# Decode and recurrence step of the sample rows moved beside gating branch and output projection, and a third projection bank in the recurrence

## Chip, cores and metric

One core of one Trainium2 chip runs the whole program. The metric is the device time of one execution in microseconds (us), lower is better. All data are float32; a large matmul is made of three passes over float32r halves ("hi" and "lo").

## What is computed

One hybrid layer is applied to a prompt of 1024 rows (1024 wide) and to 8 sample rows, each a one-token step with its own caches. After an RMS norm, `w_in` projects to three branches: A, dilated attention (12 heads of 64); B, spatial gating; C, a gated linear recurrence (6 heads, state 128 x 128 each). Their outputs, gated by silu, are joined and projected by `w_out`, and the input is added.

```python
aq, ak, av, az, bu, bv, bz, cq, cf, ci, cz = _project(xs, ...)      # the 8 sample rows
o_a = _dilated_step(aq, ak, av, cache_k[l], cache_v[l])             # 12 heads over 2048 cached rows
o_b, vn_s = _sgu(bu, bv, ...)
o_c, S_s = _hgrn2(cq, cf, ci, lb, norm_g, state_hgrn[l])            # S = f*S + k v ;  o = q S
xs = _merge(xs, o_a, az, o_b, bz, o_c, cz, w_out[l])
```

The prompt's rows go through the same functions with full attention over the dilated patterns and a recurrence over 1024 steps.

## The kernel before

The work is written in one order: `attention()` (six pairs of heads), `hgrn()` (branch C), `sgu()` (branch B), `out_proj(U)`. A scheduler moves instructions across these borders on each engine; each engine then runs its list strictly in order, and a DMA issue on SP that has to wait holds up all that stand behind it. Buffers come from tagged pools; two uses of one tag share its buffers in turn.

Weights come in blocks of 256 columns (`load_w`, L191 on): four raw tiles from SP, a high half by ACT (L205), a low half by POOL (L206). There are four buffers for high halves and four for low ones (one block), six for raw tiles. `proj_T` and `proj_nat` run 24 matmuls into a PSUM bank for one group of rows. Projections take turns on two banks (`p_proj`); the attention's transposes, the decode and the steps use the one bank of the tag "tr" (`p_tr`, `p_dk`).

`hgrn()` (L781) loops over three pairs of heads. For each it projects the values (pi, `c_proj_i`), query and forget gate (pc, `c_proj_qf`) and the output gate (pcz, `c_proj_z`). `gate` (L149) and `c_proj_qf` turn projections into gates on DVE and ACT (L152 reads a bank on DVE). `c_head` (L664) then runs the recurrence in eight blocks of 128 steps: decays (G, H), products per level (T, L648 to L656), small matmuls lv and ls, masked copies into cmat (L723 to L730), the output po, the next state S (L741), a norm pn.

After each head come the sample rows' parts. `c_step(h)` (L763) loads for all 8 rows the value row, broadcast to 128 partitions (vb), and the state (ss), forms f*S + k v on DVE (L772 to L774), writes the new state out, and multiplies by the queries (pd) on PE; `to_columns` (L754) turns the result. `decode(p)` (L924) handles two attention heads of the sample rows: for each half of the rows it loads three tiles of cached keys (dk) and the query (dqb), multiplies and sums on DVE (L950, L951), takes the softmax over partitions by small transposes (pmx, pmb) and a sum (pdn), then loads three tiles of cached values per half (dv) and multiplies (pda). Its tiles and the steps' have the tag "pq" (five buffers).

`sgu()` projects bv, then for each half of the columns bz and bu, and mixes (mx). `out_proj` (L982) takes four blocks of 256 output columns; each has eight row blocks of 48 matmuls (po). The halves yh and yl of the joined rows are made anew in each block on ACT, DVE and POOL (L1047, L1048). The first rows' tiles y0 to y7 come from DRAM by SP (L1010), the rest as yb (L1016). The sample rows' own product (pon, pos) is spread over blocks 0 to 2, with the raw weights of the block that follows.

Of the kernel before, what the change touches and what calls it, by code (L numbers as in the profile page):

```python
# [8 lines left out]
F32 = mybir.dt.float32  # L9
# [82 lines left out]
def hybrid_step(tc, ins, outs, parts=("A", "D", "B", "C", "O"), dbg=None):  # L92
    nc = tc.nc
    dbg = dbg or {}
# [4 lines left out]
    def mm(out, lhsT, rhs, start, stop):  # L99
        nc.tensor.matmul(out, lhsT=lhsT, rhs=rhs, start=start, stop=stop)  # L100

    with tc.tile_pool(name="const", bufs=1) as cp, tc.tile_pool(name="sb", bufs=1) as sb, \
# [478 lines left out]
        def c_proj_qf(h):  # L581
            blk = load_w([(OFF_CQ + h * P, P), (OFF_CF + h * P, P)], f"cqf{h}")
            f, q, kk = inp(f"f{h}"), inp(f"q{h}"), inp(f"k{h}")
            for j, dst in ((1, kk), (0, q)):
                for c in range(3):
                    ps = p_proj(f"pc{h}_{j}_{c}")
# [18 lines left out]
            qw = small(f"qs{h}", 5 * NS, tag="qs", bufs=2)  # L605
            nc.gpsimd.memset(qw[:, 3 * NS:], 0.0)
            qs = qw[:, 0:3 * NS].rearrange("p (a b) -> p a b", a=3)
            for i, x in enumerate((q, f, kk)):
                nc.scalar.copy(qs[:, i, :], x[:, S:L])
            return q, f, kk, qw  # L610

        def c_proj_i(hp):
            blk = load_w([(OFF_CI + hp * NW, NW)], f"ci{hp}")
            st = proj_nat_s(blk, f"ci{hp}")
            nc.sync.dma_start(qkv_d[3, :, hp * NW:(hp + 1) * NW], st)
            V = [inp(f"V{hp}_{j}", (P, NT, P)) for j in range(2)]
            for g in range(4):
                ps = p_proj(f"pi{hp}_{g}").rearrange("p (a b) -> p a b", a=2)
# [6 lines left out]
        def c_proj_z(hp):  # L625
            blk = load_w([(OFF_CZ + hp * NW, NW)], f"cz{hp}")
            Z = [inp(f"cz{hp}_{j}") for j in range(2)]
            for j in range(2):
                for c in range(3):
                    ps = p_proj(f"pcz{hp}_{j}_{c}")  # L630
# [33 lines left out]
        def c_head(h, q, f, kk, qw, V, z, At, lmask, dmask):  # L664
# [89 lines left out]
        def to_columns(rows, nm):  # L754

            sb_ = pq(f"{nm}s", (P, 2, P))
            nc.scalar.copy(sb_, rows[:, 0:256].rearrange("p (a b) -> p a b", a=2))
            pt = p_tr(nm)
            for i in range(2):
                nc.tensor.transpose(pt[:, i * P:(i + 1) * P], sb_[:, i, :], ident)  # L760
            return pt[:, 0:256].rearrange("p (b c) -> p b c", c=32)

        def c_step(h, q, f, kk, qw):  # L763

            qs = qw[:, 0:3 * NS].rearrange("p (a b) -> p a b", a=3)
            pd = p_tr(f"pd{h}")
            for b4 in range(2):
                bs = slice(4 * b4, 4 * b4 + 4)
                vb, ss = (pq(f"{n}{h}_{b4}", (P, 4, P)) for n in ("vb", "ss"))
                nc.sync.dma_start(vb, qkv_d[3, bs, h * P:(h + 1) * P].partition_broadcast(P))  # L770
                nc.sync.dma_start(ss, st_in[h][:, bs])
# [3 lines left out]
                nc.sync.dma_start(st_new[h][:, bs], ss)  # L775
                for b_ in range(4):
                    b = 4 * b4 + b_
                    mm(pd[32 * b_:32 * b_ + 32, b4 * P:(b4 + 1) * P], qw[:, b:b + 32], ss[:, b_, :], True, True)
            nc.scalar.copy(osT[:, h, :], to_columns(pd, f"pdt{h}s")[:, :, 0])

        def hgrn():  # L781
# [5 lines left out]
            At = [(cm[:, 256 * j:256 * j + 256], cm[:, 512 + 64 * j:576 + 64 * j]) for j in range(2)]  # L787
            for hp in range(3):
# [6 lines left out]
                a = c_proj_qf(2 * hp + 1)  # L795
                c_head(2 * hp + 1, *a, V[1], Z[1], At, lmask, dmask)
                c_step(2 * hp + 1, *a)
                decode(2 * hp + 1)

            n = HC * NS  # L800
            sq = pq("ssq", (P, n))
            nc.scalar.activation(sq, osT.rearrange("p h b -> p (h b)"), AF.Square)
            pn = p_tr("pns")
            mm(pn[:, :n], ones, sq, True, True)
            nc.scalar.activation(sq, pn[:, :n], AF.Ln, scale=1.0 / P, bias=eps)
            nc.scalar.activation(sq, sq, AF.Exp, scale=-0.5)
            nc.vector.tensor_tensor(osT, osT, sq.rearrange("p (h b) -> p h b", b=NS), ALU.mult)
            nc.vector.tensor_tensor(osT, osT, gn[:, :, None].to_broadcast([P, HC, NS]), ALU.mult)
            nc.vector.tensor_tensor(ysT[:, 10:16, :], osT, zsT, ALU.mult)


        def sgu():
            triu = small("triu", P, bufs=1, tag="kg")
# [3 lines left out]
            for j in range(2):  # L817
                ps = p_tr(f"wtp{j}").rearrange("p (a b) -> p a b", a=4)
# [12 lines left out]
            rs = p_tr("rs").rearrange("p (a b) -> p a b", a=4)  # L831
# [7 lines left out]
            st6 = small("st6", NT * 12, bufs=1, tag="dsc").rearrange("p (t a b) -> p t a b", t=NT, a=2)  # L839
            for j in range(2):  # L840
# [3 lines left out]
                for g in range(4):  # L844
# [5 lines left out]
                    for i in range(2):  # L850
                        nc.vector.bn_stats(st6[:, 2 * g + i, j, :], dst[:, i, :])

# [27 lines left out]
            pst = p_tr("pst").rearrange("p (a b) -> p a b", a=4)  # L880
# [218 lines left out]
```

## Time and profile before

| | |
|---|---|
| runs, us | 1285.92 median (1281.75, 1285.92, 1287.93) |
| the profiled execution, us | 1280.37, of which the span from first to last instruction is 1278.6 |
| busy in the span, us | PE 1203.0, DVE 918.0, ACT 669.1, POOL 290.5 |
| granted TensorE clock, mean | 0.98 |

The span is the time between the first and the last instruction of that one execution; the runs' times are those of separate executions. PE is TensorE's matmuls, DVE VectorE, ACT ScalarE, POOL GpSimd, SP the engine that issues most transfers. "Busy" counts time in which an instruction of that engine was under way; a busy PE is not PE at its peak. Stretches are named by microseconds from the span's start: attention's last pair ends near 545, the recurrence's small matmuls run from 569 to 992, the gating branch to 1079, the output projection to the end.

### The profile page before, as it was taken

The numbers are of one execution on the slowest core, as the hardware profiler recorded it, in microseconds if no ns is written. First come the engines' busy times: TensorE is split into PE (matmuls) and PEld (weight loads), VectorE is DVE, ScalarE is ACT, GpSimd is POOL, SyncE is SP. The second block draws the span as 40 slices with busy tenths as digits, with TensorE's granted clock in tenths as the row PEclk, the third lists the DMA queues.
The fourth block names the chain that finished last, engine by engine and source line by source line (L and its number), as shares of the span: only waits on it lengthen the run. The fifth ranks groups of instructions, "written<-read, shape, count | busy, mean of one in ns | idle before, by whom it ended". The sixth has DMA issues, their size and how long they took to land.

```text
span 1278.6 us, 27722 instructions
## 1 busy us (share of the span) xinstructions
PE 1203.0 (94%) x10610; PEld 1116.9 (87%) x10610; DVE 918.0 (72%) x2424; ACT 669.1 (52%) x1512; POOL 290.5 (23%) x272
## 2 busy tenths in 40 slices
PE   3899999999999998998999889998999999999998
PEld 2799888998899988987988878887989899899998
DVE  3945888668875886789897898989796534654643
ACT  4445555765548455575445554665433252454543
POOL 3531202312203121122012121111011254122221
PEclk9999999999899998998999989999999999999999
DMA  6151222312223141042253515424243224521110
GB/s 229 35 164 34 65 56 79 108 38 66 69 69 100 42 120 50 22 110 79 68 156 92 136 42 146 128 80 114 80 141 98 84 79 138 190 82 43 63 47 29
DMA packets 165044, 114.17 MB, mean 89 GB/s; under 512 B 13944, under 2 KB 158992, under 8 KB 164912
## 3 DMA queue, kind: packets, MB, share of 16 engines
q1 hardware_dynamic: 157520, 110.28, 29.4%
q10 hardware_dynamic: 6816, 1.54, 0.6%
q8 instruction: 83, 1.36, 0.4%
q0 software_dynamic: 576, 0.58, 0.3%
q14 instruction: 49, 0.40, 0.1%
HBM read 84.47 MB, written 22.09 MB: 83 GB/s over the span
## 4 chain that ended last, share of the span: by engine, by line
PE 71%; DVE 15%; issue 5%; DMA 5%; ACT 3%; SPq 1%; POOL 0%; ACTq 0%; DVEq 0%; POOLq 0%
PE po L100 15%; PE pqk L100 10%; PE pv L100 9%; PE paz L100 5%; PE pi L100 4%; PE pbu L100 4%; PE pbz L100 4%; PE pcz L100 3%; PE pbv L100 3%; PE st L100 3%; PE pc L100 3%; DMA dk<-in_cache_k_dram 3%; PE s L100 2%; DVE T L654 1%; DVE T L648 1%
## 5 line engine op out<-in xcount | busy, mean ns | idle before, releaser
L100 PE MATMUL pqk<-wh_qk,h 128*128 128x256 f32 x768 | 154.9, 292 | 5.0 <-DVE sd_qk L274 1.3
L100 PE MATMUL pc<-h,wh_cqf 128*128 128x344 f32 x576 | 144.6, 331 | 10.0 <-DVE cz L152 8.8
L100 PE MATMUL po<-woh,yh 128*128 128x256 f32 x512 | 144.3, 282 | 0.2 <-ACT yh L1047 0.2
L100 PE MATMUL po<-woh,yl 128*128 128x256 f32 x512 | 144.4, 282 | 0.0
L100 PE MATMUL po<-wol,yh 128*128 128x256 f32 x512 | 143.7, 281 | 0.0
L100 PEld LDWEIGHTS pqk<-wh_qk,h 128*128 128x128 f32 x768 | 126.0, 195 | 14.3 <-issue 3.2
L100 PEld LDWEIGHTS pc<-h,wh_cqf 128*128 128x128 f32 x576 | 102.0, 193 | 13.1 <-DVE cz L152 9.6
L100 PE MATMUL pqk<-wl_qk,h 128*128 128x256 f32 x384 | 111.3, 290 | 0.0
L100 PEld LDWEIGHTS po<-woh,yl 128*128 128x128 f32 x512 | 96.4, 188 | 3.0 <-issue 1.7
L100 PEld LDWEIGHTS po<-woh,yh 128*128 128x128 f32 x512 | 96.5, 188 | 2.0 <-ACT yh L1047 2.0
L100 PEld LDWEIGHTS po<-wol,yh 128*128 128x128 f32 x512 | 96.5, 188 | 0.0
L100 PE MATMUL pc<-h,wl_cqf 128*128 128x344 f32 x288 | 95.1, 332 | 0.0
L456 DVE CUSTOM_DVE_ANT_0 s<-s,masks 128x512 f32<-128x512 f32 (+2 forms) x144 | 77.6, 576 | 19.0 <-PE s L100 17.8
L100 PE MATMUL pi<-wh_ci,h 128*128 128x256 f32 x384 | 79.4, 301 | 12.3 <-DVE cmat L723 8.1
L100 PEld LDWEIGHTS pi<-wh_ci,h 128*128 128x128 f32 x384 | 65.1, 204 | 15.3 <-ACT dsc L963 5.4
L100 PEld LDWEIGHTS pqk<-wl_qk,h 128*128 128x128 f32 x384 | 74.9, 195 | 1.3 <-issue 0.2
L100 PE MATMUL pv<-wh_v,h 128*128 128x256 f32 x384 | 73.7, 284 | 0.0
L100 PE MATMUL pcz<-h,wh_cz 128*128 128x344 f32 x288 | 71.3, 326 | 0.2 <-DVE q L152 0.2
L100 PE MATMUL paz<-h,wh_az 128*128 128x344 f32 x288 | 69.2, 323 | 0.0
L1048 DVE TENSOR_TENSOR yl<-yb,yh 128x512 fp32r<-128x512 f32 x44 | 30.2, 690 | 53.0 <-ACT yh L1047 53.0
L100 PEld LDWEIGHTS pv<-wh_v,h 128*128 128x128 f32 x384 | 60.7, 189 | 1.8 <-issue 0.7
L1047 ACT CAST yh<-yb 128x512 fp32r<-128x512 f32 x64 | 39.5, 620 | 43.0 <-PE po L100 43.0
(388 smaller groups left out, 3586.2 us busy)
## 6 DMA issues: line engine op xcount, KB each, us to landing
wro<-in_w_out_dram SPq DMA_DIRECT2D x32, 256.0 KB
wr_qk<-in_w_in_dram SPq DMA_DIRECT2D x48, 128.0 KB
wr_cqf<-in_w_in_dram SPq DMA_DIRECT2D x48, 128.0 KB
dk<-in_cache_k_dram SPq DMA_DIRECT2D x24, 192.0 KB
dv<-in_cache_v_dram SPq DMA_DIRECT2D x24, 192.0 KB
xt<-in_x_prompt_dram SPq DMA_DIRECT2D x8, 512.0 KB
xr<-in_x_prompt_dram SPq DMA_DIRECT2D x32, 128.0 KB
out_o_yp_dram<-xr SPq DMA_DIRECT2D x32, 128.0 KB
```

Of the source, the lines that this page charges most:

```text
L100: nc.tensor.matmul(out, lhsT=lhsT, rhs=rhs, start=start, stop=stop)
L456: nc.vector.tensor_tensor_reduce(out=ps[:, :w], in0=ps[:, :w], in1=nmask[:, S - n + c:S - n + c + w], op0=ALU.add, op1=ALU.max, scale=1.0, ...
L648: nc.vector.tensor_tensor(K.rearrange("p (n w) -> p n w", w=w), g3[:, :, w - 1:w].to_broadcast([P, 4 * n, w]), h3, ALU.subtract)
L654: nc.vector.tensor_tensor(Q[:, 0:3], Q[:, 0:3], q4[:, 1:4], ALU.mult)
L1047: nc.scalar.copy(yh[:, sl, :], y)
L1048: (nc.gpsimd if piece == 0 else nc.vector).tensor_tensor(yl[:, sl, :], y, yh[:, sl, :].bitcast(F32), ALU.subtract)
```

## The change

- **Sample rows move.** `c_step` and `decode` become generators (`c_steps`, `decodes`) cut into stages by `yield`. `stages` makes a function `point()` that advances both by one stage; it is called after each group of bv (8 times), of bz and bu (24 times) and after each row block of the output projection (32 times). A decode has eight stages; a step starts every third point from the ninth on. Their PE instructions are pinned behind what was written before them on PE; what is written later may still be put ahead.
- **Buffers.** The steps' tiles take the tag "s2" (six buffers), `to_columns` the tag "e"; decodes within the output projection take "big". A step's product and state update are done by ACT (`activation` with Copy and a scale) and one DVE instruction for each row. The decode's memsets go from POOL to DVE. The queries' columns of all heads lie in the mask tile.
- **Three banks.** In `hgrn` each third projection group takes the bank "tr" (`p_turn`). The output gate pcz is projected before pc.
- **Output.** The sample rows' product is made in blocks 2 and 3 of the projection; for blocks 0 and 1 the raw weights are loaded again in block 3 (16 transfers of 256 KB), and block 3's own weights are loaded from the fourth row pair on.

The core of the diff:

```diff
+        def p_turn(nm):
+            turn[0] += 1
+            return p_tr(nm) if turn[0] % 3 == 0 else p_proj(nm)
...
-        def c_step(h, q, f, kk, qw):
-            pd = p_tr(f"pd{h}")
-            for b4 in range(2):
-                vb, ss = (pq(f"{n}{h}_{b4}", (P, 4, P)) for n in ("vb", "ss"))
...
-                nc.vector.tensor_tensor(vb, vb, qs[:, 2, bs, None].to_broadcast([P, 4, P]), ALU.mult)
-                nc.vector.tensor_tensor(ss, ss, qs[:, 1, bs, None].to_broadcast([P, 4, P]), ALU.mult)
-                nc.vector.tensor_tensor(ss, ss, vb, ALU.add)
...
+        def c_steps(qs):
+            for _ in range(8):
+                yield
+            for h in range(HC):
+                X = []
+                for b4 in range(2):
+                    vb, ss = (s2(f"{n}{h}_{b4}", shape=(P, 4, P)) for n in ("vb", "ss"))
+                    nc.sync.dma_start(vb, qkv_d[3, bs, h * P:(h + 1) * P].partition_broadcast(P))
+                    nc.sync.dma_start(ss, st_in[h][:, bs])
+                    for b_ in range(4):
+                        nc.scalar.activation(vb[:, b_, :], vb[:, b_, :], AF.Copy, scale=qs[:, 2, h, b:b + 1])
+                        nc.vector.scalar_tensor_tensor(ss[:, b_, :], ss[:, b_, :], qs[:, 1, h, b:b + 1], vb[:, b_, :],
+                                                       ALU.mult, ALU.add)
+                    nc.sync.dma_start(st_new[h][:, bs], ss)
+                yield
+                yield
+                pd = p_pv(f"pd{h}")
...
+                        pin(mm(pd[32 * b_:32 * b_ + 32, b4 * P:(b4 + 1) * P], qf[:, c:c + 32], X[b4][:, b_, :], True, True))
+                yield
+                nc.scalar.copy(osT[:, h, :], to_columns(pd, f"pdt{h}s", p_pv)[:, :, 0])
...
             for hp in range(3):
                 V = c_proj_i(hp)
-                a = c_proj_qf(2 * hp)
                 Z = c_proj_z(hp)
-                c_head(2 * hp, *a, V[0], Z[0], At, lmask, dmask)
-                c_step(2 * hp, *a)
-                decode(2 * hp)
...
+                for j in range(2):
+                    h = 2 * hp + j
+                    a = c_proj_qf(h, qs)
+                    c_head(h, *a, V[j], Z[j], At, lmask, dmask)
...
         def decode(p):
-            nc.gpsimd.memset(sc, NEG)
+            nc.vector.memset(sc, NEG)
             for bb in range(2):
...
+                yield
             nc.vector.tensor_reduce(mx[:, 0:16], sc.rearrange("p k a -> p a k"), AX.X, ALU.max)
+            yield
+            V = list(rows(ins["cache_v"], qkv_d[2], 0, "dv"))
             pt = p_dk(f"pmx{p}")
-            nc.tensor.transpose(pt[0:16, 0:P], mx[:, 0:16], ident)
+            pin(nc.tensor.transpose(pt[0:16, 0:P], mx[:, 0:16], ident))
...
+                if bb == 0:
+                    V = list(rows(ins["cache_v"], qkv_d[2], 1, "dv"))
+                yield
...
+        def stages(lanes):
+            def point():
+                for g in list(lanes):
+                    if next(g, lanes) is lanes:
+                        lanes.remove(g)
+            return point
...
+                    if nb == 3 and t < 6:
+                        for i in range(8 * t // 6, 8 * (t + 1) // 6):
+                            for b in range(2):
+                                raw = sb.tile([P, 2, NW], F32, tag="raw", name=f"wrs_{b}_{i}", bufs=N_RAW)
+                                nc.sync.dma_start(raw, w_o[:, k0:k0 + 2, b * NW:(b + 1) * NW])
...
+        attention()
+        qs = hgrn()
+        point = stages([decodes(), c_steps(qs)])
+        U = sgu(point)
+        out_proj(U, point)
```

How the order of instructions changes is shown at three places. Names are the program's, with the tile's own numbers behind; a row is line, operation, output, inputs and shape.

**PE, last pair of the attention, head 0.** Before (pc is a projection of the recurrence; st and pv are scores and products of the attention):

```order
L100 MATMUL pc_1_0_6567<-h_80,wh_cqf_0_6536 128x344
L100 MATMUL pc_1_0_6567<-h_82,wh_cqf_0_6536 128x344
L100 MATMUL pv_0_0_5982<-ph_0_0_0_5989,vh_1_4733 65x512
L100 MATMUL pv_0_0_5982<-ph_0_0_0_5989,vl_1_4734 64x512
L100 MATMUL pc_1_0_6567<-h_80,wl_cqf_0_6537 128x344
L100 MATMUL pc_1_0_6567<-h_80,wh_cqf_0_6536 128x344
L100 MATMUL pc_1_0_6567<-h_82,wh_cqf_0_6536 128x344
```

The same place now:

```order
L99 MATMUL st_0_1_0_6027<-QQ_0_5859,KK_0_5857 128x512
L464 MATMUL pm_0_1_5977<-ident,M_0_1_5951 4x128
L99 MATMUL pv_0_0_5982<-ph_0_0_0_5989,vh_1_4733 65x512
L99 MATMUL pv_0_0_5982<-ph_0_0_0_5989,vl_1_4734 64x512
L99 MATMUL st_0_1_0_6027<-Q_0_5860,K_0_5858 128x512
L99 MATMUL pv_0_0_5982<-pl_0_0_0_5986,vh_1_4733 65x512
```

The projections between the attention's matmuls are gone from here; the next one stands behind the last pm of head 1.

**PE, gating branch, first half of bu.** Now (pd is step 1, pda decode 1; dv are its value tiles of the first half of the rows):

```order
L99 MATMUL pbu_0_1_12574<-h_81,wh_bu_2_12484 128x344
L99 MATMUL pd_12463<-ss_0_12367,cmat 32x128 x4
L99 MATMUL pd_12463<-ss_1_12380,cmat 32x128 x4
L99 MATMUL pbu_0_0_12496<-h_81,wl_bu_2_12485 128x344
```

```order
L99 MATMUL pbu_0_0_12496<-h_81,wl_bu_3_12491 128x344
L99 MATMUL pda_12522<-dv_0_0_12348,dsc_12185 32x128 x4
L99 MATMUL pda_12522<-dv_0_1_12350,dsc_12185 32x128 x4
L99 MATMUL pda_12522<-dv_0_2_12353,dsc_12185 32x128 x4
L765 MATMUL pdt1s<-ident,pdt1ss 128x128 x2
L99 MATMUL pbu_0_1_12574<-h_83,wh_bu_2_12484 128x344
```

Before, only pbu and mx stood here; the steps and decodes stood within pc, pi and pcz.

**SP, start of the output projection.** Before:

```order
L1016 DMA yb_13756<-y_scr 128x8x128
L1016 DMA yb_13756<-y_scr 128x12x128 x2
L1010 DMA y_13704<-y_scr 128x4x128
L1000 DMA wro_6_13790<-in_w_out_dram 128x2x256
L1000 DMA wro_7_13794<-in_w_out_dram 128x2x256
```

Now (y is y5, the last of the eight tiles; dqb and dk belong to decode 4; wro are weights of block 1):

```order
L1061 DMA yb_13604<-y_scr 128x12x128 x2
L969 DMA dqb_0_13732<-qkv_scr 128x4x128
L957 DMA dk_0_0_13734<-in_cache_k_dram 128x4x128
L957 DMA dk_0_1_13738<-in_cache_k_dram 96x4x128
L959 DMA dk_0_1_13738<-qkv_scr 1x4x128
L1045 DMA wro_6_13638<-in_w_out_dram 128x2x256
L1045 DMA wro_7_13642<-in_w_out_dram 128x2x256
L1055 DMA y_13552<-y_scr 128x4x128
```

The load of y5 has moved behind the first loads of decode 4 and two weight tiles.

## Rows read from the trace of the kernel before

**Rows 1.** The page, busy us, share of the span and instructions

```profile
PE 1203.0 (94%) x10610; PEld 1116.9 (87%) x10610; DVE 918.0 (72%) x2424; ACT 669.1 (52%) x1512; POOL 290.5 (23%) x272
```

**Rows 2.** Stages: length, busy PE, PEld, DVE, ACT, POOL, clock, DMA share, GB/s

```profile
467.00:545.00 78.00, 72.62 (x501) 67.56 (x500) 54.43 (x127) 42.99 (x86) 12.57 (x10) 0.96 0.22 59
...
569.00:992.00 423.00, 392.86 (x4345) 359.75 (x4344) 363.59 (x1091) 219.65 (x531) 69.56 (x60) 0.96 0.38 107
992.00:1079.00 87.00, 87.00 (x610) 81.51 (x608) 34.10 (x58) 26.72 (x55) 37.60 (x28) 1.00 0.27 83
1079.00:1279.00 200.00, 196.01 (x1700) 186.62 (x1697) 111.48 (x266) 98.48 (x248) 43.67 (x32) 1.00 0.27 85
```

**Rows 3.** The same view, two windows of 4 us within the recurrence

```profile
744.00:748.00 4.00, 2.24 (x24) 1.24 (x22) 4.00 (x10) 3.98 (x10) 3.36 (x3) 1.00 0.03 7
748.00:752.00 4.00, 0.00 (x0) 0.00 (x0) 4.00 (x8) 2.76 (x6) 3.42 (x2) 0.63 0.54 150
```

**Rows 4.** Timeline of POOL and of DVE there: start, length, instruction

```profile
744.64 6.78 POOL L206 TENSOR_TENSOR wl_ci<-wr_ci,wh_ci 128x512 fp32r<-128x512 f32 x4 [28.32 <-ACT wh_ci L205]
...
749.20 1.09 DVE L655 TENSOR_TENSOR T<-T,dec 128x64 f32<-128x64 f32 x1
```

**Rows 5.** DVE by line: shapes, count, busy us, mean ns, idle before

```profile
L950 DVE TENSOR_TENSOR dk<-dk,dqb 128x512 f32<-128x512 f32 (+2 forms) x36 | 23.9, 684 | 8.5 <-DMA dk<-in_cache_k_dram 8.5
L951 DVE TENSOR_REDUCE dsc<-dk 128x8 f32<-128x512 f32 (+2 forms) x36 | 23.5, 674 | 0.0
...
L655 DVE TENSOR_TENSOR T<-T,dec 128x64 f32<-128x64 f32 x72 | 21.2, 310 | 0.0
...
L741 DVE SCALAR_TENSOR_TENSOR S<-S,eL,ls 128x128 f32<-128x128 f32 x42 | 14.2, 339 | 7.2 <-PE po L100 6.6
...
L773 DVE TENSOR_TENSOR ss<-ss,qs 128x512 f32<-128x512 f32 x12 | 9.9, 835 | 0.5 <-DMA ss<-in_state_hgrn_dram 0.4
...
L772 DVE TENSOR_TENSOR vb<-vb,qs 128x512 f32<-128x512 f32 x12 | 8.2, 690 | 4.4 <-DMA vb<-qkv_scr 2.8 <-ACT qs L609 1.5
L774 DVE TENSOR_TENSOR ss<-ss,vb 128x512 f32<-128x512 f32 x12 | 8.2, 681 | 0.0
```

**Rows 6.** Waits of PE: who waited for whom, us, times, longest

```profile
PE pc L100 <- DVE cz L152: 8.8, 3, 3.7
```

**Rows 7.** The chain that ended last: start, us, what, matmul records

```profile
89.45 22.72 PE paz L100 x144
...
567.40 0.60 PE pd L100 x14
...
711.66 6.29 DMA dk<-in_cache_k_dram
...
963.05 0.79 PE pda L100 x22
...
1087.38 6.05 DMA y<-y_scr
...
1135.53 50.25 PE po L100 x418
```

**Rows 8.** 494 to 530 us: all engines as in rows 2, then PE's pc, pi

```profile
494.00:530.00 36.00, 36.00 (x252) 34.32 (x252) 25.73 (x63) 18.96 (x41) 5.09 (x4) 1.00 0.12 31
...
494.00:530.00 36.00, 21.00 (x112) 1.00 0.12 31
...
494.00:530.00 36.00, 6.92 (x47) 1.00 0.12 31
```

**Rows 9.** Windows as in rows 2, while keys of decode 0 load

```profile
568.00:572.00 4.00, 4.00 (x27) 3.83 (x28) 4.00 (x6) 3.00 (x9) 3.57 (x4) 1.00 0.87 249
```

**Rows 10.** Timeline of SP and of DVE, step 5's value row

```profile
909.60 0.37 SPq L770 DMA_DIRECT2D vb<-qkv_scr  x1
...
913.28 0.69 DVE L772 TENSOR_TENSOR vb<-vb,qs 128x512 f32<-128x512 f32 x1 [1.66 <-DMA vb<-qkv_scr]
```

**Rows 11.** Timeline of SP at the start of the output projection

```profile
1076.66 10.62 SPq L1016 DMA_DIRECT2D yb<-y_scr  x7
```

More of the change, by code (lines that the diff above doesn't have):

```diff
@@ L99, in mm @@
     def mm(out, lhsT, rhs, start, stop):
-        nc.tensor.matmul(out, lhsT=lhsT, rhs=rhs, start=start, stop=stop)
+        return nc.tensor.matmul(out, lhsT=lhsT, rhs=rhs, start=start, stop=stop)
+    pin = tc.keep_in_program_order
     with tc.tile_pool(name="const", bufs=1) as cp, tc.tile_pool(name="sb", bufs=1) as sb, \
@@ L838, in sgu @@
             v_s = s2b("v_s", shape=(NS, CB))
-            st6 = small("st6", NT * 12, bufs=1, tag="dsc").rearrange("p (t a b) -> p t a b", t=NT, a=2)
+            st6 = small("st6", NT * 12, bufs=1, tag="kg").rearrange("p (t a b) -> p t a b", t=NT, a=2)
             for j in range(2):
@@ L851, in sgu @@
                         nc.vector.bn_stats(st6[:, 2 * g + i, j, :], dst[:, i, :])
+                    point()
             for g in range(4):
@@ L922, in hybrid_step @@
             tc.keep_in_program_order(nc.scalar.dma_start(cns[nm], ins[nm]))
+        late = [False]
         def decode(p):
@@ L927, in decode, with dk @@
             ch = slice(p * P, (p + 1) * P)
-            def dk(nm, shape=(P, 4, P)):
-                return pq(nm, shape)
+            def dk(nm):
+                return (wk if late[0] else pq)(nm, (P, 4, P))
             def rows(cache, new, bb, nm):
@@ L979, in decode, with decodes, out_proj @@
             nc.vector.tensor_tensor(ysT[:, p, :], ysT[:, p, :], mx[:, 0:NS], ALU.mult)
-        def out_proj(U):
+        def decodes():
+            for p in range(HA // 2):
+                yield from decode(p)
+        def stages(lanes):
[4 more added lines that the diff above has]
+            return point
+        def out_proj(U, point):
+            late[0] = True
             w_o = ins["w_out"][0].rearrange("(k p) n -> p k n", p=P)
@@ L991, in load_wo @@
                 for i in range(8):
+                    if nb == 3:
+                        i = (i + 3) % 8
                     if nb % 2:
@@ L1002, in load_wo @@
                     (nc.vector if nb else nc.gpsimd).tensor_tensor(lo, raw, hi.bitcast(F32), ALU.subtract)
-                    W += [(hi[:, j, :], lo[:, j, :], raw[:, j, :]) for j in range(2)]
-                return W
+                    W += [(2 * i + j, hi[:, j, :], lo[:, j, :], raw[:, j, :]) for j in range(2)]
+                return [w[1:] for w in sorted(W, key=lambda w: w[0])]
             y_v = y_d.rearrange("(k p) s -> p k s", p=P)
@@ L1031, in out_proj @@
                 Wn = load_wo(nb + 1) if nb < 3 else None
-                psn = p_st(f"pon{nb}")
+                if nb >= 2:
+                    psn = [p_st(f"pon{nb}_{i}") for i in range(2)]
                 for t in range(NT):
+                    again = []
+                    if nb == 3 and t < 6:
+                        for i in range(8 * t // 6, 8 * (t + 1) // 6):
+                            for b in range(2):
+                                raw = sb.tile([P, 2, NW], F32, tag="raw", name=f"wrs_{b}_{i}", bufs=N_RAW)
+                                k0 = order[2 * i]
+                                nc.sync.dma_start(raw, w_o[:, k0:k0 + 2, b * NW:(b + 1) * NW])
+                                again.append((b, i, raw))
                     ps = p_proj(f"po{nb}_{t}")
@@ L1056, in out_proj @@
                     nc.sync.dma_start(y_p[ts_, cs], xr)
[L1057 to L1074 removed]
+                    if nb == 2:
+                        ks = [2 * ((t + 3) % 8) + j for j in range(2)]
+                        rows8(psn[0], [(ysT[:, order[k], :], W[k][i].bitcast(F32)) for k in ks for i in range(2)], 4 * t, 2 * KO)
+                        rows8(psn[1], [(ysT[:, order[k], :], Wn[k][2]) for k in ks], 2 * t, KO)
+                    for b, i, raw in again:
+                        rows8(psn[b], [(ysT[:, order[2 * i + j], :], raw[:, j, :]) for j in range(2)], 2 * i, KO)
+                    if (nb, t) in ((2, 7), (3, 5)):
+                        for i in range(2):
+                            out_s(nb % 2 * -2 + 2 + i, psn[i])
+                    point()
+                W = Wn
+        attention()
[3 more added lines that the diff above has]
+        out_proj(U, point)
 _INS = ["x_prompt", "x_sample", "cache_k", "cache_v", "state_hgrn", "norm_g", "w_in", "q_norm_g", "k_norm_g",
```

121 lines of the change are left out of this document (52 added, 69 removed).

## Prediction

> **What bounds the kernel now.** I read the page's busy table first: PE is busy 1203.0 of 1278.6 us [rows 1], so at most some 75 us of plain idle time can be won. A share over the whole run says little here, so I cut the span into stages by the windows view [rows 2]. Gating branch and output projection are bound by PE: it is busy 87.0 of 87 us and 196.0 of 200 us at clock 1.00, while DVE is busy 34.1 and 111.5. The recurrence is not: in its 423 us PE is busy 392.9, DVE 363.6, and the granted clock averages 0.96. Its two levels are 1.2 and 2.4 GHz, so 0.96 means that 8% of the stretch, 34 us, ran at the lower one, where half of the time, 17 us, is lost. With 30.1 us idle that is **47 us lost in the recurrence**, the pool from which this change can win.
>
> What one such loss looks like is in the windows around 748 us [rows 3]: PE falls to 2.24 and then 0.00 busy of 4 us and the mean clock to 0.63, while DVE is busy 4.00 of 4.00. The timeline says why DVE is late [rows 4]: POOL makes four low halves of weights from 744.64 to 751.42, and within it the product T of 64 columns takes DVE 1.09 us, where the mean of its 72 is 0.310 [rows 5]. PE waits for DVE because a projection's PSUM bank comes free when DVE has read it: 8.8 us in three waits at pc alone [rows 6].
>
> **The change, part by part.** *Work that leaves the recurrence.* On DVE the decode's 36 products and 36 sums and the steps' three lines: 23.9 + 23.5 + 9.9 + 8.2 + 8.2 = 73.7 us [rows 5], all in the stretch but the first step's. That is a fifth of DVE's 363.6. On PE 288 records of pda at 0.79/22 = 0.036 us (10.3 us), 96 of pd at 0.60/14 = 0.043 (4.1 us) [rows 7], and some 60 small transposes and sums, 2 to 4 us by prices near these: up to 18 us. PE's part is only moved: it adds to stages in which PE has no gap, so it counts nothing in the sum. The decodes' POOL memsets become 12 on DVE (48 and 90 columns), in stages where DVE has room: nothing.
>
> *The third bank.* With it PE may run one group of 24 matmuls further ahead of DVE. From the dense stretches a matmul of 256 columns takes 50.25/418 = 0.120 us and one of 344 takes 22.72/144 = 0.158 [rows 7], so each late DVE is forgiven 2.9 to 3.8 us more. The loss of [rows 3] is 1.76 + 4.00 us of idle time; that pays for half of it or more, before the clock falls. Bounds of both together: nothing (POOL still holds DVE up) to all 47. I take three quarters, **-36 us**, nearer the upper end because a fifth of DVE's work and one bank's lateness go at once. What is late next is then DVE at the recurrence's own products, and PE itself.
>
> *The attention's end.* The third bank is the one tag that the attention's transposes use too. Group 1 of pi0 takes it and stands behind the last pm of pair 5; until pi0 is done its four weight buffers are not free, and pcz0 and pc0 cannot start. The order shows it: no projection stands between head 0's scores and head 1's last score. Before, 112 records of pc and 47 of pi stood within 494 to 530 us [rows 8]: 112 x 0.158 + 47 x 0.120 = 23.3 us of work goes out of this stretch. It can shrink to DVE's 25.7 busy us of 36 [rows 8], by 10.3, and by some 5 more as the forget gate's DVE work leaves with pc. So 8 to 13 us are lost; decode 0's scores, now on DVE just ahead, and waiting there for their loads, can add a few. Bounds 0 to 20; I take **+10 us**.
>
> *The branch stage.* Here stand now decodes 1 to 3 and all six steps. DVE gets three sixths of 23.9 + 23.5, and 48 products of 128x128 in place of the steps' lines, priced by the row of S, the same form and shape, 0.339 us [rows 5]: 24 + 16 = 40 us on top of 34.1 in about 105 us (87 plus 18 moved). It has room on average. ACT takes over the steps' scaling and has 60 free us of 87 [rows 2]. The queue and the transfers are the narrow place. Their sizes follow from the shapes: a decode loads 3.1 MB, a step moves 1.6 MB, so 9.4 + 9.4 MB join the stage's own 83 GB/s x 87 us = 7.2 MB: 26 MB in 105 us, 250 GB/s, where a window of the same loads moved 249 at a share of 0.87 [rows 9]. It fits with little left. Each pinned pd stands in PE's stream behind a state tile that was loaded after the step before had let go of its buffer; the matmuls of pbz and pbu behind it wait with it, and wr_bu1 and wro_0 wait behind the same loads on SP. The order gives PE 52 to 78 matmuls between steps, 8 to 12 us; the landing took 3.7 us [rows 10], ACT and DVE some 3 more, so mostly it holds. The last V tile of each half decode is asked for at the first half's products and needed 3 to 4 us on: a wait of some 1 us in decodes 1 to 3. Bounds 0 to +30; I take **+8 us**.
>
> *Output projection.* Decodes 4 and 5 find the queue and DVE half empty [rows 2]; a row block of 48 matmuls, 5.8 us, lies between the loads of the last V tile and its use: nothing. The sixteen re-loads of w_out, 4.2 MB, come beside 48 us of matmuls in the last block: nothing, unless a raw buffer is late. The 160 sample-row matmuls only change block. But y5, for whose landing the projection's second row block waited 6.05 us [rows 7], now stands on SP behind six more transfers, 1.2 MB, two of them waiting for raw buffers; and PE reaches it a little earlier, as pon and pos are gone from ahead of it. 1.2 MB at the 249 GB/s of [rows 9] are 5 us; the load is asked for behind 4.2 MB of yb as before [rows 11]. Bounds 0 to +9; I take **+4 us**.
>
> **Sum** against the profiled execution of 1280.37 us: -36 + 10 + 8 + 4 = -14, 1266. The median of the runs, 1285.92, lies 5.5 above it, so I predict **1272 us**. 0.5% is 6.4 us here, about what a measurement of this kernel can tell from no change.
>
> **The rivals.**
> *The lock stays.* The stalls sit where POOL casts, and the casts are as many as before. If DVE's load was not what made them long, the gain is a quarter, 12 us, the other terms add 22, and the time is 1286 - 12 + 22 = 1296; with half the gain it is 1284. For it speaks that no decode work stands next to the slow product of [rows 4]; against it that what PE lacked there was a bank. The Trainium skill ("SBUF — State Buffer", "Who interferes with whom") says that a DVE instruction with two SBUF inputs and a GpSimd instruction that reads SBUF hold their common port exclusively, the loser waiting for the whole instruction. By that rule the slow products stay slow, and come into the branch stage too, which is this rival; the stretched product of [rows 4], 1.09 us against 0.310, agrees.
> *The sample rows fall behind in the branch stage* (slower). Place: pd of each step in pbz and pbu. Under load a tile landed after 6.29 us [rows 7] instead of 3.7. A step's chain is then 0.5 to issue, 6.3 to 8 to land, 3 to compute, 1 to copy out: 11 to 12.5 us against the 8 to 12 that the order leaves. It decides from a landing of about 6.5 us: then PE loses 3 us at each of six steps and as much again as its clock drops after such gaps [rows 3], and wr_bu1 comes late: +30 in place of +8, 1294.
> *DVE is freed altogether.* PE becomes the bound of the recurrence, all 47 us go, and the attention's end costs 5: 1286 - 47 + 17 = 1256; with nothing lost at the branch 1248.
> *It does not do what it says*: the pinned stages drift to the end of the branch, as the pins set only what they follow. The order shows them spread over the stages, so I give it no chance.
>
> **How the numbers follow.** Forecast 0.36 (its own range 1262 to 1280), DVE freed 0.14, lock stays 0.30 (two thirds of it within 0.5%, a third slower), sample rows late 0.20. Faster: 0.36 + 0.14 = 0.50. Same: 0.20. Slower: 0.10 + 0.20 = 0.30. The range leaves out the top of the two bad cases together and the bottom of the good one: 1246 to 1304.
>
> **What would show it.** Right: the recurrence (first pk to the last pn) shrinks from 423 us to about 370 (18 of it moved), its clock is above 0.98, and 4 us windows with PE under 1 us busy are rare; the branch grows from 87 to about 113. Right on the attention's end: PE idle between head 0's scores and head 1's last score, pc0 done later than 569 us. Wrong: windows like those of [rows 3] as many as before (the lock), or PE waits at pd and pda of over 3 us each (the loads), or a wait for y5 well over 10 us.

## The result, and the profile after

The changed kernel takes 1313.93 us (median, 1309.54 to 1317.12), the kernel before 1284.9 us in the same series: ratio 1.024, 95% interval 1.021 to 1.027. It is **slower by 2.4%**; 1272 was forecast, and 1314 lies above the range. The profiled execution took 1317.12 us, its span is 1315.4, 36.8 more than before.

The page's first row answers to [rows 1]:

```profile
PE 1221.3 (93%) x10610; PEld 1128.6 (86%) x10610; DVE 915.3 (70%) x2448; ACT 681.6 (52%) x1560; POOL 283.1 (22%) x254
```

It has hardly moved, so the stages are read again, as in [rows 2]. The windows view of the kernel after, cut at the work itself: last pair of the attention (first pi to last pv), the projections behind it, recurrence (first pk to last pn), gating branch, output projection. Columns: length, busy PE, PEld, DVE, ACT, POOL, clock, DMA share, GB/s.

```profile
462.60:541.00 78.40, 67.68 (x410) 57.63 (x411) 58.01 (x138) 36.05 (x73) 6.96 (x6) 0.83 0.26 71
541.00:594.90 53.90, 53.90 (x340) 53.42 (x339) 23.89 (x42) 27.70 (x56) 11.86 (x11) 1.00 0.21 59
594.90:970.30 375.40, 356.32 (x3935) 333.51 (x3934) 306.44 (x959) 213.74 (x514) 61.09 (x44) 0.98 0.20 58
970.30:1088.40 118.10, 106.84 (x870) 95.20 (x868) 64.48 (x156) 42.37 (x113) 35.97 (x27) 0.93 0.67 189
1088.40:1315.40 227.00, 210.43 (x1807) 194.22 (x1806) 130.58 (x311) 98.98 (x249) 45.54 (x33) 0.97 0.41 121
```

The reader is to see that the two stages which PE filled before (87.0 of 87 us, 196.0 of 200) now have 11 and 17 us of idle time and a clock under 1.00. To compare stages whose work has moved, I count PE's **loss** as in the prediction: idle time plus (1 - granted clock) x length, summed over windows of 4 us between the same landmarks (the projections between the last pv and the first pk, which lose 2.8 us at most, are left out). Of each kernel in this study, in us:

| kernel | attention's end | recurrence | branch | output | span |
|---|---|---|---|---|---|
| before | 8.8 | 47.3 | 0.0 | 3.8 | 1278.6 |
| after | 24.4 | 25.9 | 19.8 | 23.4 | 1315.4 |
| two_banks | 11.2 | 23.6 | 19.0 | 21.8 | 1299.2 |
| bank_from_hp1 | 11.2 | 27.1 | 19.0 | 22.0 | 1300.1 |
| before_bank | 21.0 | 127.3 | 0.0 | 7.5 | 1369.8 |
| before_out | 8.9 | 47.2 | 0.0 | 14.1 | 1292.7 |
| out_late | 21.8 | 24.6 | 18.5 | 17.4 | 1310.3 |
| y5_early | 22.0 | 24.9 | 17.5 | 8.0 | 1297.7 |
| steps_out | 22.0 | 24.3 | 5.5 | 43.2 | 1316.9 |
| steps_out2 | 21.4 | 25.9 | 2.7 | 22.6 | 1300.8 |
| steps_stay | 8.6 | 43.5 | 5.5 | 17.0 | 1307.4 |
| decodes_stay | 8.8 | 47.0 | 9.1 | 11.2 | 1298.6 |
| lag | 21.5 | 23.7 | 13.5 | 17.9 | 1308.3 |
| two_y5 | 8.8 | 28.1 | 20.1 | 7.2 | 1290.7 |
| lag_best | 8.6 | 28.0 | 15.1 | 14.6 | 1295.0 |
| spread | 10.7 | 24.3 | 13.1 | 18.3 | 1292.7 |
| best | 8.9 | 24.5 | 10.3 | 26.0 | 1306.3 |
| best_wl | 11.6 | 24.3 | 7.2 | 21.1 | 1296.8 |

Before to after: +15.6 - 21.4 + 19.8 + 19.6 = +33.6 of the 36.8 us; some 3 us are more busy time. The recurrence did win; three other stages lost more.

Two limits of this table. Each row is one execution: ahead of the first pi, where PE runs the same 3255 matmuls in the same order in all eighteen, the loss still lies anywhere from 38 to 46 us, so a difference of some 4 us between two rows shows little by itself. And the four columns need not explain the span: they add up to 9.8 us more in the run named best than in the kernel before, while its span is 27.7 us longer; most of the rest is longer busy time of PE.

What PE waited for, in the view of waits (us, times, longest; rows between are left out):

```profile
...
PE po L99 <- ACT yh L1102: 9.4, 2, 8.9
...
PE pbz L99 <- DVE u L153: 4.1, 1, 4.1
PE ls L99 <- DVE cz L755: 3.2, 1, 3.2
...
PE pda L99 <- DMA dv<-in_cache_v_dram: 2.3, 2, 1.6
```

The 8.9 us are one wait, at the second row block of the output projection. The timelines of SP and of ACT show what it waits behind:

```profile
1084.45 10.66 SPq L1061 DMA_DIRECT2D yb<-y_scr  x7
1095.20 2.65 SPq L969 DMA_DIRECT2D dqb<-qkv_scr  x1
1097.95 1.38 SPq L957 DMA_DIRECT2D dk<-in_cache_k_dram  x2
1099.38 0.58 SPq L959 DMA_DIRECT2D dk<-qkv_scr  x1
1100.06 0.90 SPq L1045 DMA_DIRECT2D wro<-in_w_out_dram  x2
1101.05 0.42 SPq L1055 DMA_DIRECT2D y<-y_scr  x1
```

```profile
1104.52 0.62 ACT L1046 CAST woh<-wro 128x512 fp32r<-128x512 f32 x1 [12.46 <-DMA wro<-in_w_out_dram]
...
1106.72 0.62 ACT L1102 CAST yh<-y 128x512 fp32r<-128x512 f32 x1 [0.72 <-DMA y<-y_scr]
```

Behind yb stand decode 4's loads, two weight tiles of block 1 and y5. ACT stands 12.46 us at the weight tile with y5's rounding behind it, and then 0.72 us more until y5 lands: y5 is what comes last.

### The profile page after: what moved, and what is told of

It is laid out like the page before. It is cut to its first block, busy times and chain, and to the rows that moved or that the text cites. A ratio compares the mean times of both kernels' runs of the same rounds, so it can differ in the third digit from the quotient of the medians.

```text
span 1315.4 us, 27817 instructions
## 1 busy us (share of the span) xinstructions
PE 1221.3 (93%) x10610; PEld 1128.6 (86%) x10610; DVE 915.3 (70%) x2448; ACT 681.6 (52%) x1560; POOL 283.1 (22%) x254
## 5 line engine op out<-in xcount | busy, mean ns | idle before, releaser
L99 PE MATMUL po<-woh,yh 128*128 128x256 f32 x512 | 147.7, 289 | 9.4 <-ACT yh L1102 9.4
L99 PE MATMUL pc<-h,wh_cqf 128*128 128x344 f32 x576 | 141.2, 327 | 1.2 <-ACT k L600 1.2
L99 PEld LDWEIGHTS pqk<-wh_qk,h 128*128 128x128 f32 x768 | 125.8, 195 | 14.6 <-issue 2.9
L99 PEld LDWEIGHTS pc<-h,wh_cqf 128*128 128x128 f32 x576 | 99.1, 188 | 3.3 <-ACT k L600 1.9
L99 PE MATMUL pc<-h,wl_cqf 128*128 128x344 f32 x288 | 92.0, 324 | 0.0
L99 PEld LDWEIGHTS pi<-wh_ci,h 128*128 128x128 f32 x384 | 65.7, 206 | 11.1 <-DVE q L153 3.3
L99 PE MATMUL pcz<-h,wh_cz 128*128 128x344 f32 x288 | 68.6, 323 | 1.3 <-ACT V L627 1.3
L495 ACT ACTIVATE st<-st 128x512 f32<-128x512 f32 (+2 forms) x84 | 43.5, 538 | 36.9 <-PE st L99 35.8
```

Of the source, the lines that this page charges most:

```text
L99: return nc.tensor.matmul(out, lhsT=lhsT, rhs=rhs, start=start, stop=stop)
L495: nc.scalar.activation(st[:, :o], st[:, :o], AF.Exp, scale=E ** -0.5)
```

## Experiments

Each is the changed kernel with one edit unless its text says otherwise. Ratios are to the kernel before in the same series.

**Third bank.** The edit of two_banks, and the line of bank_from_hp1 in its place (`three` is set at the head of each pass of `hgrn`, to `hp > 0`):

```diff
-            return p_tr(nm) if turn[0] % 3 == 0 else p_proj(nm)
+            return p_proj(nm)
...
+            return p_tr(nm) if turn[0] % 3 == 0 and three[0] else p_proj(nm)
```

> The changed kernel with the recurrence's projections on two banks again. Theory (the bank "tr" costs the attention's end its fillers, and the recurrence gained because DVE's work left it): loss of PE (idle time and low clock) in the attention's last pair falls from 25.6 us to about 10, the recurrence keeps its 26 us, time 1314 - 15 = 1299 us. Rival (the recurrence gained by the third bank): the last pair is repaired all the same, but the recurrence's loss goes back to about 47 us, time 1314 - 15 + 21 = 1320 us.

> The changed kernel with the third bank only from the second pair of heads on, where no transposes of the attention are left. Theory (DVE's relief made the gain): the attention's end repaired as with two banks, recurrence within 4 us of the two-bank kernel, 1299 us. Rival (the bank made it): two thirds of the recurrence's gain of 21 us stand with the bank, so 14 us faster than the two-bank kernel.

Measured: two_banks 1303.15 us, 1.017 (1.014 to 1.021); bank_from_hp1 1302.44, 1.015 (1.012 to 1.019). Both theories hold, the rivals do not. The attention's end is repaired, and the recurrence loses 23.6 us with two banks against 25.9 with three: the bank gave nothing there that these rows can show, and 27.1 with the bank back from the second pair on says the same.

before_bank is the kernel before with `p_turn` alone (so too for pc, pcz and pss_ci):

```diff
-                ps = p_proj(f"pi{hp}_{g}").rearrange("p (a b) -> p a b", a=2)
+                ps = p_turn(f"pi{hp}_{g}").rearrange("p (a b) -> p a b", a=2)
```

> The kernel before with the third bank in the recurrence alone (each third projection group in the bank tr), decode, steps and output as before. Theory (the bank is of no use to the recurrence and takes the attention's end its fillers): PE's loss in the last pair of the attention rises from 9 to 20 us or more, the recurrence's stays within 6 us of 47, time 1284 + 12 = 1296 us or more, the more so as the decode waits for the bank too. Rival (the prediction's own: the bank forgives DVE's lateness in the recurrence): the recurrence's loss falls by 15 us or more, time 1284 or less.

Measured: 1369.97 us, 1.068 (1.065 to 1.071). Windows of attention's end and recurrence:

```profile
464.20:536.90 72.70, 63.59 (x396) 53.11 (x397) 49.18 (x124) 36.51 (x73) 5.80 (x6) 0.84 0.18 48
585.10:1065.80 480.70, 401.12 (x4290) 362.85 (x4287) 358.69 (x1081) 218.63 (x517) 67.38 (x60) 0.90 0.33 94
```

The attention's end loses 12 us more, as the theory had it. The recurrence, which it had left at 47, loses 80 more: here decode and steps use that bank too. PE's longest waits there stand in the decode's chain and at the recurrence's own lv; in the kernel before neither pdn nor lv has a wait above 0.5 us in that stage:

```profile
PE pdn L100 <- DVE dmx L971: 14.0, 3, 4.9
PE lv L100 <- DVE T L662: 13.3, 10, 5.6
```

That the shared bank ties these chains together fits, but no run takes it apart.

**Output projection.** before_out is the kernel before with the changed `out_proj`, whose stages are not called:

```diff
-                    rows8(psn, [(ysT[:, order[k], :], Wn[k][2]) for k in (2 * t, 2 * t + 1)], 2 * t, KO)
+                if nb == 2:
+                    ks = [2 * ((t + 3) % 8) + j for j in range(2)]
...
+                for b, i, raw in again:
```

> The kernel before with the changed output projection alone: the sample rows' product in blocks 2 and 3 with the weights loaded again, no stage called, decode and steps where they were. Theory (in the kernel before, the some 100 small matmuls of that product stood between the first two row blocks and covered the wait for y5): a wait of about 6 us at the second row block with a low clock behind it, time 1284 + 8 = 1292 us. Rival (the stall of the changed kernel is made by decode 4's loads alone, the product covered nothing): within 3 us of 1284.

Measured: 1295.62 us, 1.008 (1.005 to 1.012): the theory holds. Its wait of PE:

```profile
PE po L100 <- ACT yh L1059: 5.2, 1, 5.2
```

In the kernel before, ACT waited for y5 for 9.0 us, and PE had other work meanwhile (waits of ACT from 1080 us, PE's only wait in the stage; PE by line, 1086.8 to 1093.6 us):

```profile
ACT yh L1047 <- DMA y<-y_scr: 9.0, 1, 9.0
PE po L100 <- ACT yh L1047: 0.2, 1, 0.2
```

```profile
L100 PE MATMUL pos<-woh,ysT 128*8 128x256 f32 x31 | 4.2, 379 | 0.0
L100 PE MATMUL pos<-wol,ysT 128*8 128x256 f32 x31 | 3.8, 379 | 0.0
```

out_late calls the stages later and pins decode 4's loads; y5_early gives y5 another buffer besides:

```diff
-                    point()
+                    if 8 * nb + t >= 4:
+                        point()
...
-            YT = [s2(f"y{i}", shape=(P, 4, P)) if i < 6 else ee(f"y{i}", (P, 4, P)) for i in range(8)]
+            YT = [s2(f"y{i}", shape=(P, 4, P)) if i < 5 else (pq if i == 5 else ee)(f"y{i}", (P, 4, P)) for i in range(8)]
```

> The changed kernel with the stages called in the output projection only from its fifth row block on, and decode 4's key loads pinned on SP there. Theory (block 1's last weight tiles and y5 land late because decode 4's loads stand ahead of them, behind the 3.1 MB of yb): PE's wait of 8.9 us at the second row block falls under 3 us and the low clock behind it goes, the output projection's loss falls from 23 to about 8 us, time about 1299 us. Rival (yb alone holds the queue): the wait stays at 6 us or more, time 1310 us.

> The kernel of out_late, and y5 in a buffer of the tag pq, so that its load stands ahead of yb on SP and its rounding ahead of block 1's last two weight tiles on ACT. Theory (the 6.3 us at the second row block are the time until y5 and those two tiles land behind yb's 3.1 MB): the wait falls under 2 us and the low clock behind it goes, output projection's loss from 17.4 to about 9 us, time 1304 us. Rival (the transfers' rate holds the block whatever comes first): the wait moves to the next row block with the same length, 1310 us or more.

Measured: out_late 1312.49 us, 1.024 (1.021 to 1.027), its wait 6.3 us: by these two executions decode 4's loads made 2.6 of the 8.9, and the rival holds for the rest. y5_early 1302.02, 1.014 (1.011 to 1.017): the wait is gone, as the theory had it. What is left of PE's waits in its output projection, and the stage's window:

```profile
PE po L99 <- DVE yl L1105: 1.9, 4, 1.3
```

```profile
1081.50:1297.70 216.20, 208.49 (x1807) 192.05 (x1806) 127.70 (x311) 99.06 (x249) 50.08 (x33) 1.00 0.42 126
```

**Gating branch.** The edit of steps_out, and what steps_out2 adds to it:

```diff
-        point = stages([decodes(), c_steps(qs)])
+        lanes = [decodes()]
+        point = stages(lanes)
         U = sgu(point)
+        lanes.append(c_steps(qs))
```

```diff
-                    vb, ss = (s2(f"{n}{h}_{b4}", shape=(P, 4, P)) for n in ("vb", "ss"))
+                    vb, ss = (pq(f"{n}{h}_{b4}", (P, 4, P)) for n in ("vb", "ss"))
...
-                yield
                 yield
                 pd = p_pv(f"pd{h}")
```

> The changed kernel with the six recurrence steps' stages called from the output projection's row blocks instead of the gating branch (the sample rows' product takes its rows in another order for it). Theory (DVE and ACT stand at the steps' loads in the branch, ahead of the reads that free its PSUM banks): the branch's loss falls from 20 us to about 8, DVE's waits for ss and ACT's for vb are gone from it, time about 1302 us. Rival (the decodes' key loads do it): branch loss stays above 15 us, 1310 to 1316 us. If the steps do in the output projection what they did in the branch, 1314 us with the loss moved there.

> As steps_out, with the steps' tiles in the tag pq instead of s2, whose six buffers y0 to y5 hold all through the output projection, and a step at every second point: the steps now stand in blocks 0 to 2 on PE instead of block 3. Theory (the loss of 43 us in the output projection of steps_out was the steps held back to block 3): branch loss about 5.5 us, output projection's loss back to 23 to 26 us, time 1302 us. Rival (the transfers of steps and decodes collide with yb there as they did in the branch): 1312 us or more.

Measured: steps_out 1316.25 us, 1.026 (1.022 to 1.030): branch as in the theory (5.5), the loss moved to the output projection. steps_out2 1301.78, 1.014 (1.011 to 1.017): the theory's numbers came; since the edit also makes a step one point shorter, how much of it the buffers alone did is not shown. DVE's and ACT's waits in the branch of the kernel after:

```profile
DVE dk L971 <- DMA dk<-in_cache_k_dram: 13.2, 5, 5.0
DVE ss L783 <- DMA ss<-in_state_hgrn_dram: 11.6, 4, 3.7
DVE ss L783 <- ACT pdt3ss L762: 4.6, 1, 4.6
```

```profile
ACT vb L782 <- DMA vb<-qkv_scr: 20.8, 7, 7.4
```

and in steps_out2, where the rows of ss and vb are gone and the clock is 1.00:

```profile
DVE dk L968 <- DMA dk<-in_cache_k_dram: 9.2, 4, 4.7
```

```profile
963.00:1061.70 98.70, 95.98 (x775) 87.75 (x773) 56.36 (x113) 28.24 (x60) 36.09 (x27) 1.00 0.53 151
```

lag keeps every byte and moves only the waiting instructions (the step's in the same way):

```diff
-                for kind, n, t in rows(ins["cache_k"], qkv_d[1], bb, "dk"):
-                    nc.vector.tensor_tensor(t[0:n], t[0:n], qb[0:n], ALU.mult)
+                K = list(rows(ins["cache_k"], qkv_d[1], bb, "dk"))
+                yield
+                for kind, n, t in K:
+                    pin(nc.vector.tensor_tensor(t[0:n], t[0:n], qb[0:n], ALU.mult))
```

> The changed kernel with the sample rows' loads one stage ahead of their use: a step's ACT and DVE instructions and a decode's key products are pinned behind the work of the next stage on their engines; the same transfers, three banks, y5 as changed. Theory (the branch's loss comes from where DVE and ACT stand at loads, ahead of the reads that free its banks): DVE's waits for ss and dk in the branch fall from 30 us to under 12, the branch's loss from 20 to about 8 us, time 1302 us; the attention's end also gains some us, since decode 0's products leave it. Rival (26 MB in the branch are too many whatever stands where): the waits move to pd and pda on PE, the branch's loss stays above 15 us, 1311 us or more.

Measured: 1307.21 us, 1.019 (1.017 to 1.022); branch 13.5, between the two numbers. DVE no longer waits for the loads of ss (but 6.5 us there for ACT's scaling), and still 12.0 us for dk; PE now waits 4.4 us at pmx and 2.9 at pda, so in part the waits moved, as the rival had it. The place of the waiting instructions is thus about a third of the branch's loss; about half of it or more went only where the steps or the decodes left the stage.

**What relieved the recurrence.** Both from two_banks: behind each head in `hgrn`, steps_stay advances `c_steps` and decodes_stay `decodes`, unpinned.

```diff
                     c_head(h, *a, V[j], Z[j], At, lmask, dmask)
+                    for _ in range(3):
+                        next(steps)
```

> The two-bank kernel with the six steps back in the recurrence, one behind each head, not pinned, in the new form (ACT scales, one DVE instruction a row); only the decodes are stages. Theory (the decodes' 47 us of DVE work made the recurrence's gain, the steps' loads a good part of the branch's loss): branch loss from 19 to about 6 us, recurrence's loss from 24 to about 29, time 1303 - 13 + 5 = 1295 us. Rival (the steps weigh in the recurrence as much as the decodes): its loss goes to 36 us or more, 1302 us.

> The mirror of steps_stay: two banks, the six decodes back in the recurrence, one behind each head, not pinned; only the steps are stages, all in the branch. Theory after steps_stay (what costs PE in the recurrence is any of the sample rows' work beside it, the steps' as much as the decodes'): the recurrence's loss at 40 us or more, branch at 8 to 12 us, time 1305 us. Rival (steps_stay lost for the form of its steps, which put 15 us of scaling on ACT ahead of the rounding of keys; the decodes alone cost little): recurrence's loss under 32 us.

Measured: steps_stay 1309.77 us, 1.021 (1.018 to 1.024), recurrence 43.5: its theory falls, the rival holds (its time, 1302, is 8 us short). decodes_stay 1302.25, 1.015 (1.013 to 1.018), recurrence 47.0: the theory holds. Either half, put back, takes nearly the whole gain with it. No one wait explains it: PE's longest rows in the stage are 7.5 us (po, at cmat of DVE) and 7.2 (pk, at ki of ACT) in steps_stay, 3.9 (pcz, at cz of DVE) and 3.8 (pc, at k of ACT) in decodes_stay. The branch loses 5.5 us with the decodes alone, 9.1 with the steps alone, 19.8 with both. The recurrence's windows of steps_stay, then of decodes_stay:

```profile
578.40:979.60 401.20, 369.76 (x3999) 342.75 (x4000) 309.94 (x978) 227.25 (x552) 61.46 (x44) 0.97 0.23 66
```

```profile
575.70:995.60 419.90, 386.47 (x4182) 360.47 (x4181) 330.54 (x1051) 224.07 (x530) 71.43 (x48) 0.97 0.28 82
```

DVE is busy for 77% and 79% of these, and for 82% of the recurrence of the kernel after, which loses half as much. So DVE's busy share is not what decides. A share falls when a stage gets longer, but against the stage's length less PE's loss it is the same picture: 0.87 and 0.89 here, 0.88 in the kernel after.

**Repairs together.** two_y5 is two_banks with y5_early; lag_best adds lag; spread instead puts a step at every sixth point (pq tiles in the output projection); best is two_banks, steps_out2 and y5_early with stages from the third row block; best_wl makes the low halves of the recurrence on DVE. Of spread and of best_wl:

```diff
+                for _ in range(3 if h < HC - 1 else 0):
+                    yield
```

```diff
-                nc.gpsimd.tensor_tensor(lo, raw, hi.bitcast(F32), ALU.subtract)
+                low.tensor_tensor(lo, raw, hi.bitcast(F32), ALU.subtract)
```

> The repairs of the attention's end and of the output projection together: two banks and the kernel of y5_early; steps and decodes in the branch as changed. If the terms add: 1314 - 12 - 12 = 1290 us, with PE losses of about 10 (attention's end), 24 (recurrence), 18 (branch), 8 (output projection). Rival (as in best, what is repaired comes back as a wait elsewhere): 1298 us or more.

> The kernel of two_y5 with the loads one stage ahead as in lag: every term repaired where it arose, and no work moved to another stage. If the terms add: 1290 less 10 to 12 of the branch = 1279 us, a little faster than before (1284). Rival (the stages' pins on DVE and ACT hold these engines in the output projection or the recurrence): 1290 us or more.

> The kernel of two_y5 with a step at every sixth point instead of every third: four steps in the branch, two in the output projection (tiles of the tag pq there). Theory (the branch's loss grows with how close the steps and decodes stand, since DVE and ACT then wait at loads that land late): the branch's loss falls from 20 to about 11 us, the output projection gains 2 us of PE work, time 1292 - 9 + 2 = 1285 us, level with before. Rival (the decodes' key loads and value loads make the branch's loss, however the steps stand): 1291 us or more.

> All repairs in one: two banks; the steps in the output projection (pq tiles, every second row block); stages there from the third row block on, the first loads of decode 4 and of step 0 pinned behind it on SP; y5 in pq. If the terms add: the changed kernel's 1314 less 12 (bank, attention's end), less 12 to 14 (steps out of the branch), less 10 to 12 (y5 and its stall) = 1277 us, slightly faster than before (1284): PE losses of about 11 (attention's end), 24 (recurrence), 3 (branch), 8 (output projection). Rival (the loads that are moved out of the stalled places collide anew in the output projection): loss there above 18 us, 1287 us or more.

> The kernel best with the low halves of the recurrence's twelve weight blocks (48 instructions) made by DVE instead of POOL. Theory (what is left of the recurrence's loss comes from POOL's bursts of four, beside which DVE's products of two inputs run three times as long): the long products of T are gone, the recurrence's loss falls from 24 to about 14 us although DVE takes 48 x 0.69 = 33 us more work, 10 us faster than best. Rival (DVE's own load is what is late): slower than best by 5 us or more.

Measured: two_y5 1292.16 us, 1.006 (1.004 to 1.008): the terms add. lag_best 1296.26, 1.010 (1.008 to 1.012), and spread 1294.49, 1.011 (1.009 to 1.013), are no faster than two_y5, as their rivals' times had it, though the branch did gain (5.0 and 7.0): the output projection lost 7.4 and 11.1 for it. best 1306.37, 1.018 (1.015 to 1.020): its rival holds. best_wl 1300.28, 1.014 (1.011 to 1.016): the recurrence's loss stays (24.5 and 24.3), and the run is 6 us faster than best with intervals that just touch, so neither text holds. It does not settle the theory either: in the stage the three lines of T's later products take DVE 63.7 us against 75.0 in best, but 32 casts that now stand there take 21.8. None of these is faster than the kernel before.

In best, PE is also busier (1220.0 us against 1203.0 before). One part of it is pd; its row in the output projection of best (all 96 matmuls), then that of the whole kernel after:

```profile
L99 PE MATMUL pd<-ss,cmat 128*32 128x128 f32 x96 | 10.1, 300 | 6.2 <-DVE ss L782 6.2
```

```profile
L99 PE MATMUL pd<-ss,cmat 128*32 128x128 f32 x96 | 3.8, 278 | 0.0
```

## Why the prediction was wrong, step by step

The four terms missed by 47.6 us together: 15.6 at the output projection, 14.6 in the recurrence, 11.8 in the branch, 5.6 at the attention's end. The first lies outside its bounds; the second is nearly as large.

- **Output projection, +4 of 0 to 9: measured +19.6, the step that failed.** The prediction read 6.05 us of y's transfer in the chain of waits as a wait of the second row block, and said that PE reaches it "a little earlier, as pon and pos are gone". But PE's own wait before was 0.2 us: the sample rows' product stood there and covered it. That cover alone, taken away, costs 10.3 us of loss (before_out, +0.8%). Bounding the term by bytes (1.2 MB, 5 us) asked how much later y5 lands, not what stood in the gap. That answer was near: y5's rounding starts 18.2 us behind the branch's last mx in the kernel after, 14.2 before, 4 us later. With y5 asked for early (y5_early) the stage's loss falls to 8.0.
- **Branch, +8 of 0 to 30: +19.8.** Inside its bounds; the place named was the smaller part. The prediction looked for PE's waits at pd and pda: there are none at pd and 2.3 us at pda, with 3.4 us of low clock behind it (994 to 1002 us, below). DVE stood 25 us at loads of ss and dk and ACT 21 at vb, and behind them in their queues stood the reads that free PE's banks: pbz and pbu waited 5.8 us for DVE, again with 3.4 us of low clock behind. "It has room on average" was true of DVE's busy time (64.5 of 118 us) and told nothing.

```profile
994.30:998.30 4.00, 2.41 (x21) 1.23 (x20) 0.00 (x0) 0.94 (x4) 0.00 (x0) 0.60 1.03 274
998.30:1002.30 4.00, 4.00 (x19) 4.00 (x16) 3.81 (x10) 0.37 (x1) 0.00 (x0) 0.54 0.72 202
```

- **Attention's end, +10 of 0 to 20: +15.6.** The mechanism is as told: no fillers, pc0 done at 585.2 us (539.1 before). Of the added loss only 5.3 us are idle time (10.7 against 5.4); 10.3 (13.7 against 3.4) are the clock, which the term left out. Four windows of the kernel after:

```profile
484.00:488.00 4.00, 2.66 (x9) 2.09 (x10) 3.25 (x12) 3.99 (x7) 0.00 (x0) 0.50 0.56 147
488.00:492.00 4.00, 4.00 (x20) 4.00 (x20) 3.97 (x11) 1.45 (x3) 0.00 (x0) 0.50 0.45 116
...
508.00:512.00 4.00, 3.24 (x11) 2.29 (x11) 2.72 (x7) 2.72 (x5) 0.00 (x0) 0.50 0.00 0
512.00:516.00 4.00, 4.00 (x22) 3.02 (x23) 2.86 (x9) 0.48 (x1) 0.00 (x0) 0.50 0.02 6
```

  After a wait of 4.8 us for QQ, PE is at 1.2 GHz, and with gaps between head 0's and head 1's matmuls it falls there again.
- **Recurrence, -36 of 0 to -47: -21.4.** Length (375 for about 370) and clock (0.98) came as told, the length by luck: of the 49 us that it is shorter (landmark to landmark) 21 are loss and 28 are work, where the prediction had 36 and 18; some 9 us of the work are projections that now stand ahead of the first pk. The step "one bank's lateness" failed: the bank gave nothing, and "a fifth of DVE's work" is not the measure either, since half of it out gives hardly any of the gain. Why either half costs nearly all of it stays open.
- **The rivals.** The nearest was "sample rows fall behind" (1294), right in its stage and mostly wrong in its place: not pd on PE, but DVE and ACT. "The lock stays" told the signs to look for: about half the loss stays, and DVE's long products still stand beside POOL's casts (timelines of POOL and of DVE; a T of 192 columns takes 1.25 us here, 0.35 in most of its rows):

```profile
736.72 4.01 POOL L207 TENSOR_TENSOR wl_ci<-wr_ci,wh_ci 128x512 fp32r<-128x512 f32 x3 [20.75 <-ACT wh_ci L206]
```

```profile
737.09 2.51 DVE L659 TENSOR_TENSOR T<-T,q 128x192 f32<-128x192 f32 x2
```

  The Trainium skill ("SBUF — State Buffer", "Who interferes with whom") gives the lock behind such rows, and these rows agree. Whether the remaining 24 us hang on it stays open: in best_wl, where POOL makes none of the recurrence's low halves, the loss is the same, but there DVE has the casts themselves.
- **Range and chances.** Each of the two slower rivals moved one term and left the others at their middle, and the range left out the bad cases together. The three costs lie in different stages and have different causes, so they came together: with -36 kept, their upper ends 20 + 30 + 9 already give +23, which is 1309 for the median.

## What to carry to other kernels

Before moving work out of a stage, ask what it covered there: a transfer in the chain of waits whose consumer PE shows almost no wait was hidden by something, and that something may be what you move. An instruction put beside a PE-bound stage costs what its queue stands for, not what it is busy: look at what frees PSUM behind it on DVE and ACT. Keeping its load a stage ahead won 6 us of the branch in lag, but no time on top of two_y5. When costs have separate places, add them; do not choose among them (so did the repairs of two_y5). But look again at a stage that takes over the moved work: best saved 9.8 us of loss in the branch against two_y5 and lost 18.8 more in the output projection.

## What was not expected of the hardware

The 96 pd matmuls took 3.8 us in the kernel after, in six runs of 16 (0.64 us each), 6.1 in the kernel before, in runs of 2 (0.41) to 14 (0.64), and 10.1 in best, where nine of 18 runs are twos (0.41 us) between po's matmuls and two runs fall to the lower clock: here short matmuls were cheap only together. And a busy PE hid a lot: from 488 to 492 us it shows 4.00 of 4 us busy at half the clock.
